# Layer 1's FFN down product as seven block products instead of eight

## The chip, the cores and the metric

The program runs on one core of one Trainium2 chip. The core has five engines that each work through their own list of instructions and meet only at semaphores: TensorE (PE, with its weight loads shown as PEld), VectorE (DVE), ScalarE (ACT), GpSimd (POOL) and SyncE (SP, which here only issues DMAs). The metric is the device time of one execution in microseconds (us); lower is better. A step of 512 columns through the 128x128 array is called a matmul below. Everything is computed in fp32 from three products of rounded parts: an operand is split into a high part (a cast to fp32r) and a low part (the rest), and hi·hi, hi·lo and lo·hi are summed in PSUM. One 128x128x512 block product is therefore three matmuls.

## What is computed

Two layers (DEPTH = 2) over 1024 latent tokens of width 1024, each an attention mixer and a feed-forward block with a convolution over tokens:

```python
def conv_ffn(h, w_up, conv_w, conv_b, w_down):
    u = h @ w_up                                  # 1024 x 1024 @ 1024 x 5632
    ...
    for j in range(CONV_W):                       # 3 taps along the tokens
        acc = acc + up[:, j:j + L] * conv_w[j]
    a, g = jnp.split(acc, 2, axis=-1)             # 2816 + 2816
    return (jax.nn.silu(g) * a) @ w_down          # 1024 x 2816 @ 2816 x 1024

# per layer, latent stream:
x = layer_norm(DN_ALPHA * x + m[2] * mixer(x), ...)
x = layer_norm(DN_ALPHA * x + m[5] * conv_ffn(modulate(x, m[3], m[4]), ...), ...)
```

The change is in the last part of the last layer: the product of the gated hidden values (1024 x 2816, that is 22 blocks of 128 hidden columns) with `w_down`.

## The kernel before

Layer 1's feed-forward block is one call of `ffn2` and ends the program. It has two phases.

**Up phase.** A loop of 22 passes (`p`), one per hidden block. Each pass makes the 128 `a` and the 128 `g` columns of its block by seven block products of 12 matmuls (`product`, L1689) into the PSUM tiles x, v, y, x, q, y, q: this product already goes by seven in place of eight. In the order of PE: W[0] into x, W[1] into v, W[4] into y, W[2] into x, W[5] into q, W[6] into y, W[3] into q. Beside it ACT casts the next pass's weights to their high parts (L1661), DVE takes the low parts (L1663) and the sums of weight blocks (L1665, L1668), ACT and DVE assemble the halves of `ua` and `ug` from the PSUM tiles (L1912, L1929 on ACT; L1921 and L1927 on DVE), and one pass later the convolution of the finished block runs: its centre tap on ACT (L1784), its side taps on DVE (L1792), SiLU on ACT (L1815), the gate product on DVE (L1818), and POOL issues the store of the 128x1024 block to `g` in DRAM (L1819). SP loads a pass's weights (L1642).

**Down phase.** 44 steps of 24 matmuls (`mm3`, L399 to L401): 22 hidden blocks for the left 512 output columns, then 22 for the right ones, each step over eight token tiles `t` with one PSUM bank each. `load` (L1763 for two blocks of `w_down`, L1767 for one block of `g`) brings a step's operands up to 8 steps ahead, and ACT and DVE split them (L110 and L111 for weights, L1773 and L1774 for `g`). The residual rows `z` come in (L1972) and are scaled (L1975, L1976). After the first 22 steps the banks are multiplied by the gate row (L1994) and added to `z` (L1962, with `bn_stats` in L1963). The last 8 steps are turned around: for each token tile in turn all 8, and then its evict (L2024, L1962, L1963) and its final norm, `finish_o`: L355 `bn_aggr`, two tiny POOL operations for the inverse deviation (L357, L358), two 128x1024 DVE operations (L2418, L2421) and the store to `out`, issued by SP (L2422).

The order of every engine's instructions is the order in which the code emits them, up to small moves by the framework's scheduler outside the parts marked `manual_schedule`; queues are served in order.

## Time and profile before

| quantity | value |
|---|---|
| median of 3 runs | 2938.8 us (2936.71 to 2944.41) |
| profiled execution | 2939.45 us |
| its span | 2937.7 us |
| mean granted TensorE clock | 0.98 |
| busy PE / DVE / ACT / POOL | 2788.0 / 2042.8 / 1365.4 / 635.5 us |
| up phase of layer 1 | ends at 2686 us from the span's start |
| down phase of layer 1 | 2686 to 2937.7 us |

In rows of the trace the first number is the start in us from the span's start, the second the duration; then engine, line, operation, output <- inputs, and in brackets the engine's idle time before it and what it waited for. Consecutive instructions overlap: the next one often starts before the printed end of the last. "x2" behind a row joins two instructions.

### The profile page before, as it was taken

The page shows a single profiled execution, that of the slowest core. Times are in us where ns is not written, and L with a number is a line of the kernel's source. Part 1 is how long each engine was busy: PE and PEld are TensorE (multiplying, and loading weights), DVE is VectorE, ACT ScalarE, POOL GpSimd, SP SyncE. Part 2 cuts the span into 40 slices and gives each one's busy share as a digit, 9 for nine tenths or more (in the row PEclk, how much of TensorE's full clock was granted, in tenths as well). Part 3 has the DMA queues.
Part 4 walks back from the last instruction along what each step waited for, and adds up shares of the span by engine and source line. Part 5 has one row for each costly group of instructions (what it writes and reads, how often), then busy time and mean ns, then how long its engine had stood idle before and what let it go on. Part 6 is the DMA issues. An engine that isn't in the chain of part 4 may idle for free.

```text
span 2937.7 us, 44921 instructions
## 1 busy us (share of the span) xinstructions
PE 2788.0 (95%) x16728; PEld 2276.0 (77%) x16728; DVE 2042.8 (70%) x3749; ACT 1365.4 (46%) x2594; POOL 635.5 (22%) x864
## 2 busy tenths in 40 slices
PE   7999899989999999999999978989998999999998
PEld 4877677778788978888888867766676788888886
DVE  4866366666578778888887566467767777777656
ACT  4321255567336655555553352267743555555330
POOL 2601233354450000000001023345543000000001
PEclk9999999999999999999999999989999999999999
DMA  8568611042667643333387427632144222225651
GB/s 263 156 193 273 215 39 34 9 157 74 171 186 224 202 153 107 119 112 113 101 302 240 144 92 228 190 95 65 52 151 158 77 75 86 86 79 189 241 161 61
DMA packets 347378, 416.47 MB, mean 142 GB/s; under 512 B 23432, under 2 KB 262312, under 8 KB 345624
## 3 DMA queue, kind: packets, MB, share of 16 engines
q1 hardware_dynamic: 326776, 351.31, 38.5%
q0 software_dynamic: 17488, 60.60, 6.0%
q8 instruction: 131, 2.15, 0.3%
q10 hardware_dynamic: 2896, 1.70, 0.2%
q14 instruction: 87, 0.71, 0.1%
HBM read 317.79 MB, written 95.75 MB: 141 GB/s over the span
## 4 chain that ended last, share of the span: by engine, by line
PE 71%; issue 9%; DVE 8%; DMA 6%; ACT 4%; POOL 1%; SPq 0%; ACTq 0%; POOLq 0%; DVEq 0%
PE q L1689 8%; PE x L1689 8%; PE y L1689 8%; PE d L399 5%; PE d L401 5%; PE d L400 5%; PE S L760 4%; PE v L1689 4%; PE pv L905 3%; PE T L891 3%; PE mm L399 2%; PE mm L401 2%; PE mm L400 2%; PE T L856 2%; PE pv L865 2%
## 5 line engine op out<-in xcount | busy, mean ns | idle before, releaser
L784 POOL TENSOR_SCALAR P<-P,rin 128x640 f32<-128x640 f32 (+3 forms) x288 | 249.5, 870 | 348.6 <-DVE rin L783 322.6
L1663 DVE TENSOR_TENSOR w<-raw,w 128x512 fp32r<-128x512 f32 x308 | 208.0, 688 | 143.1 <-ACT w L1661 143.0
L399 PE MATMUL d<-w,w 128*128 128x512 f32 x704 | 275.1, 391 | 0.0
L400 PE MATMUL d<-w,w 128*128 128x512 f32 x704 | 274.7, 390 | 0.0
L401 PE MATMUL d<-w,w 128*128 128x512 f32 x704 | 274.5, 390 | 0.0
L110 ACT CAST w<-raw 128x512 fp32r<-128x512 f32 x276 | 161.1, 620 | 185.2 <-PE d L401 128.1
L111 DVE TENSOR_TENSOR w<-raw,w 128x512 fp32r<-128x512 f32 x260 | 169.0, 691 | 97.3 <-ACT w L110 95.1
L760 PE MATMUL S<-k,q 64*128 64x256 f32 (+2 forms) x1824 | 192.9, 338 | 17.7 <-DVE nm L2248 9.2
L1819 POOL DMA_DIRECT2D g<-cv x44 | 23.5, 534 | 845.0 <-DVE cv L1818 845.0
L781 ACT ACTIVATE P<-P,nm 128x641 f32<-128x641 f32 (+4 forms) x208 | 161.3, 777 | 84.2 <-DVE nm L2248 46.9
L1661 ACT CAST w<-raw 128x512 fp32r<-128x512 f32 x308 | 182.0, 621 | 13.8 <-DVE raw L1668 7.9
L760 PEld LDWEIGHTS S<-k,q 64*128 64x128 f32 x1824 | 136.5, 189 | 53.4 <-issue 18.5
L771 ACT COPY PT<-T 128x512 f32<-128x512 f32 (+1 forms) x250 | 134.2, 567 | 77.6 <-PE T L891 75.4
L401 PEld LDWEIGHTS d<-w,w 128*128 128x128 f32 x704 | 132.6, 188 | 27.8
L400 PEld LDWEIGHTS d<-w,w 128*128 128x128 f32 x704 | 132.5, 188 | 27.5
L399 PEld LDWEIGHTS d<-w,w 128*128 128x128 f32 x704 | 132.5, 188 | 27.2
L905 PE MATMUL pv<-PT,v 128*64 128x128 f32 x2016 | 133.6, 280 | 16.7 <-ACT PT L771 13.8
L1774 DVE TENSOR_TENSOR w<-raw,w 128x512 fp32r<-128x512 f32 x176 | 112.3, 687 | 49.9 <-ACT w L1773 49.8
L891 PE MATMUL T<-ident,P 128*128 128x128 f32 x1008 | 136.1, 282 | 7.8 <-POOL P L784 3.4
L905 PEld LDWEIGHTS pv<-PT,v 128*64 128x64 f32 x2016 | 109.4, 138 | 42.5 <-ACT PT L771 22.3
L1929 ACT COPY ug<-q 128x512 f32<-128x512 f32 x44 | 25.9, 589 | 245.3 <-PE q L1689 245.3
L1773 ACT CAST w<-raw 128x512 fp32r<-128x512 f32 x176 | 98.8, 618 | 84.1 <-PE d L401 70.1
(364 smaller groups left out, 7566.2 us busy)
## 6 DMA issues: line engine op xcount, KB each, us to landing
raw<-in_up_dram SPq DMA_DIRECT2D x132, 512.0 KB
raw<-g SPq DMA_DIRECT2D x88, 512.0 KB
raw<-in_down_dram SPq DMA_DIRECT2D x66, 512.0 KB
g<-cv POOLq DMA_DIRECT2D x44, 512.0 KB, 3.0
araw<-in_ada_w_dram SPq DMA_DIRECT2D x32, 512.0 KB
raw<-in_w_in_dram SPq DMA_DIRECT2D x28, 512.0 KB
araw<-in_ada_w_dram SPq DMA_DIRECT2D x40, 256.0 KB
wt<-in_ada_w_dram SPq DMA_DIRECT2D x16, 512.0 KB
```

Of the source, the lines that this page charges most:

```text
L111: (lo_eng or nc.vector).tensor_sub(lo, s, f32(hi))
L399: nc.tensor.matmul(ps, lh, rh, start=first, stop=False)
L400: nc.tensor.matmul(ps, lh, rl, start=False, stop=False)
L401: nc.tensor.matmul(ps, ll, rh, start=False, stop=last)
L760: self.nc.tensor.matmul(outs[a], q[r, x, qs], k[r, y, ks], start=(i == 0), stop=(i == 2))
L781: nc.scalar.activation(P[:, :m], P[:, :m], AF.Exp, bias=negm, scale=-1.0, accum_out=den)
L784: nc.gpsimd.tensor_scalar(P[:, :n], P[:, :n], rin, 1.0, ALU.mult, ALU.mult)
L891: nc.tensor.transpose(ps[:, s * 128 : (s + 1) * 128], P[a][:, cols[i + x] : cols[i + x] + 128], self.ident,)
L905: nc.tensor.matmul(O[a * HD : (a + 1) * HD], v_of(a, vts[i + x]), pT[:, s * 128 : (s + 1) * 128], start=(i + x == 0), stop=(i + x == m - 1 ...
L1661: nc.scalar.copy(half(i, 0), src[i])
L1663: nc.vector.tensor_sub(half(i, 1), src[i], f32(half(i, 0)))
L1689: nc.tensor.matmul(ps, w[:, a, s], r[b][:, k], start=first and k + i == 0, stop=k == 3 and i == 2, skip_group_check=True,)
```

## The change

A new function, `ffn7`, takes the place of `ffn2` for layer 1 (layer 0 keeps `ffn2`). With the gated values in two token halves by two hidden halves, A11, A12, A21, A22 (hidden halves of 11 blocks), and `w_down` in two hidden halves by two column halves, W11, W12, W21, W22, it makes seven products in this order:

| steps | left factor (G) | right factor | PSUM banks | after it |
|---|---|---|---|---|
| 0 to 10 | S1 = A21 + A22 | V: T1 = W12 - W11 | Y | copy Y to `vs` (SBUF) |
| 11 to 21 | A11 | W11 | X | copy X to Y |
| 22 to 32 | A12 | W21 | X, summed on | X is the left columns of token tiles 0 to 3 |
| 33 to 43 | S2 = S1 - A11 | V: T2 = W22 - T1 | Y, summed on | copy Y to X |
| 44 to 54 | S4 = A12 - S2 | W22 | Y, summed on | Y + `vs` is the right columns of tiles 0 to 3 |
| 55 to 65 | S3 = A11 - A21 | V: T3 = W22 - W12 | X, summed on | X + `vs`: right columns of tiles 4 to 7; copy X to Y |
| 66 to 76 | A22 | V: W21 - T2 | Y, summed on | Y: left columns of tiles 4 to 7 |

A step is now 12 matmuls over four token tiles; there are 77 steps. X and Y are four PSUM banks each, and the copies are done by ACT.

The up phase visits the hidden blocks in pairs, one of each half (ORDER: 0, 11, 1, 12 and so on). The convolution results of a pair are the tiles `gk` and `go`. In place of one 512 KB store per block, a pair makes seven 256 KB stores to `G`, and DVE makes S1 in `store`, S3, S2 and S4 in `mix`, in place: each sum overwrites a half that an earlier store reads. The gate product stays one 128x1024 instruction. The weight sums are made by a generator, `mix_down`, that is advanced four times per pass: per pair of blocks five loads of 256 KB on SP, four DVE subtractions and four 256 KB stores to `V` on POOL, 77 advances in all, so that it is through in the 20th of the 22 passes.

In the down phase a `load` brings two steps: 512 KB of the right factor, 512 KB of G, two casts and two subtractions of 128x512 for the right factor, and from load 3 on one cast and one subtraction of 128x1024 for G. Loads lead by at most 6. The jobs of `evict` and `end` (the final norm and store of a token tile) for tiles 0 to 3 stand between steps 55 and 62; the evicts of tiles 4 to 7 (right columns) stand at steps 66 and 67; the last nine steps are turned around by token tile, four of them now.

Two small rows (`gq`, `gk` of the attention, no relation to the tile `gk`) move from one pool to another, so that their two DMAs on SP stand behind eight loads of `x` at the program's start.

```diff
+ORDER = [f + h for f in range(NF // 4) for h in (0, NF // 4)]
+            ("G", [7 * NF // 4, 128, 512]), ("V", [NF, 128, 512]),
...
+    def mix_down(self, tp, l):
+        nc, V = self.nc, self.d["V"]
+        w = self.io["down"][l].rearrange("(f p) n -> p f n", p=128)
+        HF = NF // 4
+        def load(tag, i, n):
+            r = self.t(tp, [128, 512], tag)
+            nc.sync.dma_start(r, w[:, f + i * HF, n * 512 : (n + 1) * 512])
+            return r
+        def sub(o, x, y, i):
+            nc.vector.tensor_sub(o, x, y)
+            nc.gpsimd.dma_start(V[i * HF + f], o)
+        for f in range(HF):
+            a, b = load("va", 1, 1), load("vb", 0, 1)
+            yield
+            sub(a, a, b, 2)
+            yield
+            a = load("va", 0, 0)
+            yield
+            sub(a, b, a, 0)
+            b = load("vb", 1, 1)
+            yield
+            sub(b, b, a, 1)
+            yield
+            a = load("va", 1, 0)
+            yield
+            sub(a, a, b, 3)
+            yield
...
+            def right(s, m):
+                q, f = divmod(s, HF)
+                if q in (0, 3, 5, 6):
+                    o = (0, 3, 5, 6).index(q) * HF + f
+                    return Vv[:, o : o + m]
+                o, n = {1: (0, 0), 2: (HF, 0), 4: (HF, 1)}[q]
+                return dn[:, o + f : o + f + m, n * 512 : (n + 1) * 512]
+            def raw():
+                rp.append(rp.pop(0))
+                return self.t(rp[0], [128, 2, 512], "raw")
+            def load(j):
+                s, m = 2 * j, min(2, 7 * HF - 2 * j)
+                if m <= 0:
+                    return
+                r, g = raw(), raw()
+                if m == 2 and (s + 1) % HF == 0:
+                    nc.sync.dma_start(r[:, :1], right(s, 1))
+                    nc.sync.dma_start(r[:, 1:], right(s + 1, 1))
+                else:
+                    nc.sync.dma_start(r[:, :m], right(s, m))
+                nc.sync.dma_start(g[:, :m], Gv[:, s : s + m])
+                for i, w in enumerate(self.split([r[:, i] for i in range(m)], 512)):
+                    wd[s + i] = w
+                if j < 3:
+                    for i, w in enumerate(self.split([g[:, i] for i in range(m)], 512)):
+                        ga[s + i] = w
+                    return
+                w = self.t(gp[0], [128, 2, 2, 512], "w", R)
+                nc.scalar.copy(w[:, 0, :m], g[:, :m])
+                nc.vector.tensor_sub(w[:, 1, :m], g[:, :m], f32(w[:, 0, :m]))
+                for i in range(m):
+                    ga[s + i] = w[:, :, i]
+            side = self.mix_down(up, l)
...
+                def a1(s):
+                    s.a = centre("go" if s.i % 2 else "gk", s.u[0], s.p)
+                def a2(s):
+                    sides(s.a, s.u[0], s.p)
+                def g1(s):
+                    s.g = centre("cv", s.u[1], s.p + NP)
+                def g2(s):
+                    sides(s.g, s.u[1], s.p + NP)
+                def silu(s):
+                    nc.scalar.activation(s.g, s.g, AF.Silu)
+                def store(s):
+                    f, x = s.i // 2, s.a
+                    nc.vector.tensor_mul(x, x, s.g)
+                    if s.i % 2 == 0:
+                        half["k"] = x
+                        put(1, f, x[:, :512])
+                        return
+                    put(2, f, x[:, :512])
+                    put(6, f, x[:, 512:])
+                    k = half["k"]
+                    nc.vector.tensor_add(k[:, 512:], k[:, 512:], x[:, 512:])
+                    put(0, f, k[:, 512:])
+                def mix(s):
+                    f, x, k = s.i // 2, s.a, half["k"]
+                    if s.i % 2 == 0:
+                        nc.vector.tensor_sub(k[:, :512], k[:, :512], k[:, 512:])
+                        put(5, f, k[:, :512])
+                        return
+                    nc.vector.tensor_sub(x[:, 512:], x[:, 512:], k[:, :512])
+                    put(3, f, x[:, 512:])
+                    nc.vector.tensor_sub(x[:, :512], x[:, :512], x[:, 512:])
+                    put(4, f, x[:, :512])
...
+                    call("h", 4)
+                    call("l", 3)
+                    c.store()
+                    nc.vector.tensor_tensor(v1, u1, cols(Q), ALU.add)
+                    next(side, None)
+                    self.product(W[6], b22, Y, False)
+                    call("l", 4)
+                    call("s", 5)
+                    call("s", 6)
+                    nc.vector.tensor_tensor(u1, u1, cols(Y), ALU.add)
+                    self.product(W[3], T[3], Q, False)
+                    nc.scalar.copy(v0, cols(Q))
+                    call("h", 5)
+                    call("h", 6)
+                    c.mix()
+                    next(side, None)
+                    c = conv(ua, ug, p)
+                    W, late_l = W2, call
+                for _ in side:
+                    pass
+                load(1)
+                for x in (c.a1, c.g1, c.a2, c.g2, c.silu, c.store, c.mix):
+                    x()
...
+            gp[0] = es.enter_context(self.pool("fgs", bufs=6))
...
+            X, Y = ([self.t(pd, [128, 512], f"d{x}{t}") for t in range(4)] for x in "xy")
+            banks = (Y, X, X, Y, Y, X, Y)
+            NS = 7 * HF
+            last = 9
+            def mm(i, t):
+                q, f = divmod(i, HF)
+                c = slice(t * 128, t * 128 + 128)
+                for k, (a, b) in enumerate(((0, 0), (0, 1), (1, 0))):
+                    nc.tensor.matmul(
+                        banks[q][t], ga[i][:, a, c], wd[i][:, b],
+                        start=q < 2 and f + k == 0, stop=f == HF - 1 and k == 2,
+                        skip_group_check=True,
+                    )
+            def evict(t, n, ps, v=None):
+                s = slice(n * 512, (n + 1) * 512)
+                tt = self.t(tt2, [128, 512], "tt")
+                if v is None:
+                    nc.vector.tensor_mul(tt, ps, gate[:, s])
+                else:
+                    nc.vector.tensor_add(tt, v, ps)
+                    nc.vector.tensor_mul(tt, tt, gate[:, s])
+                nc.vector.tensor_add(z[t][:, s], z[t][:, s], tt)
+                nc.vector.bn_stats(s6[t][:, n], z[t][:, s])
...
+            def end(t):
+                finish(t, z[t], s6[t])[0]()
...
+            def copies(dst, src):
+                for a, b in zip(dst, src):
+                    nc.scalar.copy(a, b)
+            job(HF - 1, copies, vs, Y)
+            job(2 * HF - 1, copies, Y, X)
+            job(4 * HF - 1, copies, X, Y)
+            job(6 * HF - 1, copies, Y, X)
+            for t in range(4):
+                job(3 * HF + 1 + 2 * t, evict, t, 0, X[t])
+                job(5 * HF + 2 * t, evict, t, 1, Y[t], vs[t])
+                job(5 * HF + 1 + 2 * t, end, t)
+                job(6 * HF + t // 2, evict, 4 + t, 1, X[t], vs[t])
+            ahead = 2
+            for i in range(NS - last):
+                if i % 2 == 0:
+                    n = i // 2 + min(5, 2 + i // 4)
+                    while ahead <= n:
+                        load(ahead)
+                        ahead += 1
+                for t in range(4):
+                    mm(i, t)
+                for f in jobs.pop(i, ()):
+                    f()
+            for t in range(4):
+                for i in range(NS - last, NS):
+                    mm(i, t)
+                evict(4 + t, 0, Y[t])
+                end(4 + t)
...
-        self.ffn2(1, h2l, [hl, pxc], {}, d["T1"], rows("x3"), a[1, 0, 5], view1, begin_o, finish_o,
-                  (io["ln_g"][1, 0], io["ln_b"][1, 0]), early=self.early, px=px, last=8, share=(9, (1, 4, 7)))
+        self.ffn7(1, h2l, [hl, pxc], {}, d["T1"], rows("x3"), a[1, 0, 5], view1, begin_o, finish_o,
+                  (io["ln_g"][1, 0], io["ln_b"][1, 0]), early=self.early, px=px)
```

On SP, at the end of the program, before (in these rows `raw` is a load's staging tile, `z` a token tile's 128x1024 rows, and the number behind a name tells tiles apart):

```order
L1763 DMA raw_28050<-in_down_dram 128x2x512
L1767 DMA raw_28058<-g_97 128x1024
L1767 DMA raw_28090<-g_97 128x1024
L157 DMA lg_28126<-in_ln_g_dram 128x1024
L157 DMA lb_28127<-in_ln_b_dram 128x1024
L2422 DMA out_dram<-z_4958_26675 128x1024
L2422 DMA out_dram<-z_4959_26676 128x1024
```

and after, in the same place (L2813 is the store of a token tile, L2120 and L2121 are the two DMAs of a load; the rows are load 33 to load 38):

```order
L2120 DMA raw_28148<-V_101 128x2x512
L2121 DMA raw_28149<-G_100 128x2x512
L2813 DMA out_dram<-z_5009_26958 128x1024
L2120 DMA raw_28198<-V_101 128x2x512
L2121 DMA raw_28199<-G_100 128x2x512
L2813 DMA out_dram<-z_5010_26959 128x1024
L2120 DMA raw_28248<-V_101 128x2x512
L2121 DMA raw_28249<-G_100 128x2x512
L2813 DMA out_dram<-z_5011_26960 128x1024
L2120 DMA raw_28298<-V_101 128x2x512
L2121 DMA raw_28299<-G_100 128x2x512
L2813 DMA out_dram<-z_5012_26961 128x1024
```

Before, no store of `out` stood ahead of a load; now four do, one ahead of each of the loads 34 to 37.

On DVE after, between two of these stores (L113 and L2130 take the low parts of load 34, L2362 to L2365 are the evict of a token tile, L357, L2809 and L2812 its final norm):

```order
L2812 SCALAR_TENSOR_TENSOR z_5009_26958<-z_5009_26958,rs_28175,lb_27618 128x1024
L2362 TENSOR_TENSOR tt_28193<-v_5026_26975,dy_5040_26995 128x512
L2363 TENSOR_TENSOR tt_28193<-tt_28193,gate_26978 128x512
L2364 TENSOR_TENSOR z_5010_26959<-z_5010_26959,tt_28193 128x512
L2365 BN_STATS s_5018_26967<-z_5010_26959 128x6
L113 TENSOR_TENSOR w_28202<-raw_28198,w_28202 128x512
L113 TENSOR_TENSOR w_28205<-raw_28198,w_28205 128x512
L2130 TENSOR_TENSOR w_28208<-raw_28199,w_28208 128x1024
L357 BN_AGGR mv_28223<-s_5018_26967 128x2
L2809 SCALAR_TENSOR_TENSOR z_5010_26959<-z_5010_26959,mv_28223,lg_27617 128x1024
L2812 SCALAR_TENSOR_TENSOR z_5010_26959<-z_5010_26959,rs_28225,lb_27618 128x1024
```

The low parts of load 34 stand ahead of the norm of token tile 1 in DVE's list; before, all splits stood ahead of every norm.

On ACT after, the end of the program (the last casts of loads 36 to 38, and the copies X to Y behind step 65):

```order
L112 CAST w_28302<-raw_28298 128x512
L112 CAST w_28305<-raw_28298 128x512
L2129 CAST w_28308<-raw_28299 128x1024
L112 CAST w_28347<-raw_28343 128x512
L112 CAST w_28350<-raw_28343 128x512
L2129 CAST w_28353<-raw_28344 128x1024
L2390 COPY dy_5039_26994<-dx_5035_26990 128x512
L2390 COPY dy_5040_26995<-dx_5036_26991 128x512
L2390 COPY dy_5041_26996<-dx_5037_26992 128x512
L2390 COPY dy_5042_26997<-dx_5038_26993 128x512
L112 CAST w_28388<-raw_28384 128x512
L2129 CAST w_28391<-raw_28385 128x512
```

Before, ACT's list ended in casts and had no copy that PE waits for in the down phase; now the copies that step 66 sums on stand behind the three casts of load 37.

On DVE in the up phase, before, from the gate product of one pass to the next pass's first split (L1818 the gate product, L1921 the half `v1`, which frees the PSUM tile q, L1927 the half `u1`):

```order
L1818 TENSOR_TENSOR cv_25009<-cv_25009,cv_25030 128x1024
L1921 TENSOR_TENSOR ug_24990<-ua_24989,q_4744_24987 128x512
L1663 TENSOR_TENSOR w_25083<-raw_24888,w_25083 128x512
L1668 TENSOR_TENSOR raw_24888<-raw_24888 128x512
L1668 TENSOR_TENSOR raw_24886<-raw_24886,raw_24888 128x512
L1927 TENSOR_TENSOR ua_24989<-ua_24989,y_4743_24986 128x512
L1663 TENSOR_TENSOR w_25118<-raw_24888,w_25118 128x512
```

and after, in a pass whose convolution ends a pair:

```order
L2181 TENSOR_TENSOR go_25153<-go_25153,cv_25174 128x1024
L2189 TENSOR_TENSOR gk_25004<-gk_25004,go_25153 128x512
L2305 TENSOR_TENSOR ug_25134<-ua_25133,q_4775_25131 128x512
L1665 TENSOR_TENSOR w_25231<-raw_25020,w_25231 128x512
L1670 TENSOR_TENSOR raw_25020<-raw_25020 128x512
L1670 TENSOR_TENSOR raw_25018<-raw_25018,raw_25020 128x512
L2311 TENSOR_TENSOR ua_25133<-ua_25133,y_4774_25130 128x512
L2198 TENSOR_TENSOR go_25153<-go_25153,gk_25004 128x512
L2200 TENSOR_TENSOR go_25153<-go_25153 128x512
L2050 TENSOR_TENSOR va_25240<-va_25240,vb_25242 128x512
L1665 TENSOR_TENSOR w_25273<-raw_25020,w_25273 128x512
```

S1 (L2189) now stands between the gate product and `v1` (L2305), S2 and S4 (L2198, L2200) and a weight sum (L2050) ahead of the next pass's split.

180 lines of the change are left out of this document (175 added, 5 removed).

## The prediction

> **What bounds the kernel now.** I read the page first, then the windows of the two phases of layer 1's feed-forward block, the chain of waits and the groups by line, and from there single stretches of the timeline. In this order, from these views:
>
> ```profile
> span 2937.7 us, 44921 instructions
> PE 2788.0 (95%) x16728; PEld 2276.0 (77%) x16728; DVE 2042.8 (70%) x3749; ACT 1365.4 (46%) x2594; POOL 635.5 (22%) x864
> ...
> 2252.00:2686.00 434.00, 422.82 (x1837) 347.26 (x1838) 321.33 (x409) 224.72 (x348) 13.66 (x24) 0.98 0.30 92
> 2686.00:2937.70 251.70, 239.45 (x1057) 197.94 (x1055) 159.28 (x223) 75.69 (x132) 15.12 (x17) 0.98 0.48 170
> ...
> 2506.57 2.72 PE q L1689 x12
> ...
> L400 PE MATMUL d<-w,w 128*128 128x512 f32 x352 | 136.9, 389 | 0.0
> ```
>
> PE is busy 95% of the span. The third and fourth rows are the up and the down phase (length; busy us and count of PE, PEld, DVE, ACT, POOL; clock; DMA share; GB/s). In the down phase PE's matmuls fill 239.45 of 251.7 us, and the group row shows 0.0 us of idle time ahead of them. The chain row gives the pitch: 12 matmuls in 2.72 us, 0.2267 us each. So a matmul taken away there is worth its pitch, as long as nothing else becomes late. What follows the last matmuls, in the timeline of the phase's end:
>
> ```profile
> 2887.41 0.69 DVE L2024 TENSOR_TENSOR tt<-d,gate 128x512 f32<-128x512 f32 x1 [8.93 <-PE d L401]
> 2888.13 0.69 DVE L1962 TENSOR_TENSOR z<-z,tt 128x512 f32<-128x512 f32 x1
> ...
> 2889.59 0.21 DVE L355 BATCH_NORM_AGGREGATE mv<-s 128x2 f32<-128x12 f32 x1
> 2889.83 1.28 DVE L2418 SCALAR_TENSOR_TENSOR z<-z,mv,lg 128x1024 f32<-128x1024 f32 x1
> 2891.85 1.28 DVE L2421 SCALAR_TENSOR_TENSOR z<-z,rs,lb 128x1024 f32<-128x1024 f32 x1 [0.73 <-POOL rs L358]
> 2893.05 0.68 DVE L2024 TENSOR_TENSOR tt<-d,gate 128x512 f32<-128x512 f32 x1
> ...
> 2926.78 0.68 DVE L2024 TENSOR_TENSOR tt<-d,gate 128x512 f32<-128x512 f32 x1
> ...
> 2931.20 1.28 DVE L2421 SCALAR_TENSOR_TENSOR z<-z,rs,lb 128x1024 f32<-128x1024 f32 x1 [0.71 <-POOL rs L358]
> ```
>
> Per token tile DVE needs 5.64 us (2887.41 to 2893.05); the norm alone, from `bn_aggr` to the end of L2421, is 3.54. The last evict and norm take 2926.78 to 2932.48, 5.70 us, and the span ends 5.2 us later with the last store. I count times from the down phase's start (2686.0); before, the last norm ends at +246.5.
>
> **The change, part by part.**
>
> *Matmuls.* 44 x 24 = 1056 become 77 x 12 = 924: 132 x 0.2267 = 29.9 us less, the whole of the possible gain.
>
> *The stores of tiles 0 to 3 among the loads.* How much of it is lost is decided by these rows, the waits of SP's queue (us in total, times, longest) and single rows of the timeline:
>
> ```profile
> SPq L2422 <- DVE z L2421: 69.5, 8, 33.0
> ...
> SPq L1642 <- DVE w L1663: 450.8, 39, 18.7
> ...
> 2724.91 0.32 SPq L1767 DMA_DIRECT2D raw<-g  x1
> 2726.16 0.32 SPq L1972 DMA_DIRECT2D z<-x  x1
> ...
> 2731.49 0.38 SPq L1763 DMA_DIRECT2D raw<-in_down_dram  x1
> ...
> 2734.75 1.15 ACT L110 CAST w<-raw 128x512 fp32r<-128x512 f32 x2 [1.52 <-DMA raw<-in_down_dram]
> ...
> 2507.09 1.07 ACT L1815 ACTIVATE cv<-cv 128x1024 f32<-128x1024 f32 x1
> ...
> 2517.49 0.57 ACT L1887 COPY y<-x 128x512 f32<-128x512 f32 x1 [1.09 <-PE x L1689]
> ...
> 2509.30 1.22 DVE L1818 TENSOR_TENSOR cv<-cv,cv 128x1024 f32<-128x1024 f32 x1
> 2510.44 0.68 DVE L1921 TENSOR_TENSOR ug<-ua,q 128x512 f32<-128x512 f32 x1
> ```
>
> SP waits at an instruction until its releaser is done, up to 33.0 us for the norm ahead of a store. Before, all stores stood behind all loads, and this cost nothing. Now a store of tile t waits on DVE for norm t, load 34 + t stands behind it on SP, load 34 + t's splits stand on DVE ahead of norm t + 1. That is a ring: each turn must run through in series.
>
> One turn, from the end of norm t: the load is issued at once behind the store; from issue to first cast 3.26 us (2731.49 to 2734.75); the store's own 512 KB go ahead, one more slot of 1.25 (2724.91 to 2726.16); G comes one slot later, 1.25; its 128x1024 cast 1.07 (the SiLU row is the nearest of that size), its low part 1.22 (the gate product's row), the norm 3.54. Sum 11.6 us, in which PE does two steps, 5.44. The evict (2.9 of DVE) fits into the wait for data.
>
> First turn: load 33's casts reuse tiles that steps 54 and 55 read, so they start when step 55 ends, at 56 x 2.72 = +152.3. One 128x512 cast 0.57, then 1.07, 1.22 and 3.54: norm 0 ends at +158.7. Norm 3 ends three turns later, at +193.5.
>
> PE meanwhile runs on loaded data to step 66, at 66 x 2.72 = +179.5. There it needs the copies X to Y, which stand on ACT behind load 37's casts, and load 37 is behind the fourth store: its G is cast at 193.5 + 3.26 + 1.25 + 1.25 + 1.07 = +200.3, the first copy takes 0.57 more (the later ones have the 0.68 that PE spends per tile). PE waits there from +179.5 to +200.9, 21.4 us. A restart is slow at first, as the timeline shows behind an earlier wait:
>
> ```profile
> 2300.68 0.69 PE L1689 MATMUL q<-T3h,w 128*128 128x512 f32 x1 [2.97 <-DVE ug L1921]
> ...
> 2304.89 0.39 PE L1689 MATMUL q<-T3h,w 128*128 128x512 f32 x1
> 2305.12 0.40 PE L1689 MATMUL x<-h3lah,w 128*128 128x512 f32 x1
> ```
>
> After this idle of 2.97 us, 12 matmuls took 4.44 us (2300.68 to 2305.12) in place of 2.72: 1.7 us. I take that once; the bounds are 0 and twice that. Steps 66 to 76 are 11 x 2.72 = 29.9, then the last evict and norm 5.7: the last norm ends at 200.9 + 1.7 + 29.9 + 5.7 = +238.2. DVE is through with the evicts of tiles 4 to 7 by then (about 202 + 4 x 2.9 = +214). Against +246.5 the down phase gains 8.3 us out of 29.9.
>
> A rule of the Trainium skill would make the ring shorter. "DMA: Bandwidth & Descriptors", section "Two DMAs through the same engine are not ordered", has it that in one queue transfers start in order but are pipelined, with reading and writing on separate queues. Then the load's reads need not wait for the store's slot, and three turns lose 3 x 1.25 us. No row here shows a store followed by a load on SP.
>
> *The first copies* (behind steps 10, 21, 43) have no late load ahead of them; each takes 0.57 against PE's 0.68 per tile: nothing; bounds 0 and 4 x 0.57 each.
>
> *The sums in the up phase.* 44 sums of halves (S1 to S4 of 11 pairs) and 44 weight sums, all 128x512, at DVE's pitch of about 0.6 us. Per pass 44 / 19.25 = 2.3 weight sums and 1 or 3 sums of halves: 2.0 or 3.2 us. These must fit DVE's gaps, in the timeline of one pass (and W[3] in the chain):
>
> ```profile
> 2500.74 2.60 DVE L1792 SCALAR_TENSOR_TENSOR cv<-ua,cc,cv 128x1023 f32<-128x1023 f32 x2 [0.46 <-ACT cv L1784]
> ...
> 2508.69 0.69 DVE L1663 TENSOR_TENSOR w<-raw,w 128x512 fp32r<-128x512 f32 x1 [1.03 <-ACT w L1661]
> ...
> 2515.91 1.29 DVE L1663 TENSOR_TENSOR w<-raw,w 128x512 fp32r<-128x512 f32 x2 [2.38 <-ACT w L1661]
> ...
> 2518.63 0.69 DVE L1663 TENSOR_TENSOR w<-raw,w 128x512 fp32r<-128x512 f32 x1 [0.82 <-ACT w L1661]
> ...
> 2512.01 2.72 PE q L1689 x12
> ```
>
> The gaps of a pass of 19.04 us are 0.46 + 1.03 + 2.38 + 0.82 = 4.7 us, all spent on ACT, so late work is caught up there. The tight place is `v1`, which frees q for W[3]: it ends at 2511.12, PE starts W[3] at 2512.01, 0.89 us later. S1 ahead of it takes 0.6 of that; the weight sum ahead of it falls into the 1.03. So I take 0 per pass; the bounds are 0 and 2.6 - 0.9 = 1.7 us per pass (all the added work late at `v1`). Only in pass 0, where DVE has no such gap, does a weight sum delay W[3]: +0.6 us.
>
> *The new transfers* are 256 KB each: per pair 7 stores and 9 transfers for the weight sums in place of 2 stores. In that phase the DMA share is 0.30 (first fence), so there is room; SP's weight loads for a pass are issued a pass ahead. Zero; bounds 0 and 0.2 per pass.
>
> *Between the phases* S2 and S4 of the last pair wait until earlier stores have landed (the page's DMA issues, with the us to landing, and the timeline):
>
> ```profile
> g<-cv POOLq DMA_DIRECT2D x44, 512.0 KB, 3.0
> ...
> 2697.32 1.23 DVE L1818 TENSOR_TENSOR cv<-cv,cv 128x1024 f32<-128x1024 f32 x1 [1.19 <-ACT cv L1815]
> ...
> 2698.84 0.53 POOL L1819 DMA_DIRECT2D g<-cv  x1 [16.55 <-DVE cv L1818]
> ```
>
> The second store of the pair would be issued about 2699.4 and land 3.0 later, +16.4. In DVE's new list the splits of loads 2 and 3 stand ahead of S2, so steps 4 to 7 have their data: zero. Behind S2 and S4 (1.2) and with their own four (2.4), load 2 would be ready at +20, 9 us after step 4's turn at +10.9: bounds 0 and 9.
>
> *The two small rows* leave SP's queue ahead of `x` (two slots of 1.25), but DVE then waits for them: 0; bounds -2.5 and +1.
>
> **Sum**: -8.3 + 0.6 = -7.7 us. The profiled execution took 2939.45, 0.65 over the median, so I set the sum against the median: 2938.8 - 7.7 = 2931.1. What a measurement can tell from no change is 0.3%, 8.8 us: below 2930.0 counts as faster, above 2947.6 as slower.
>
> **The rivals.**
> - *Reads pass the store*: a load's first data come as if no store stood ahead, turns of 10.35 us, norm 3 at +189.8, so 2927.4. Against it: the rows of transfers issued one after the other, 1.25 us apart; for it: none of those rows mixes the two directions. The Trainium skill's rule above would give this case.
> - *Stores do not hold the loads.* Then load 37 is early, the copies come at step 66 on time, and DVE bounds: per tile splits 2.4, norm 3.5, evict 2.9, so norm 3 at 158.7 + 3 x 8.8 = +185.1; splits of loads 37 and 38 (3.7) and four evicts to +200.4; then four times 5.64 to +223.0, 23.5 less: 2915.9. Against it speaks the 33.0 us wait of SP at a store.
> - *The store holds the rings longer*: with 3.0 us (the put's landing) for 1.25 a turn is 13.35, 2936.4; with the 5.2 us behind the last norm 15.6, about 2943. It loses to before from a turn of 14.2 on.
> - *DVE falls behind in the up phase* (the slower side): `v1` late in each pass because the sums don't fall into the gaps. It becomes slower than before from 7.7 / 22 = 0.35 us per pass, by over 0.3% from 0.75; at 0.8 the time is 2948.7. For it: the margin at `v1` is 0.3 us in every second pass; against: 4.7 us of gaps ahead of it.
>
> **How the numbers follow.** The forecast 0.45, reads pass 0.10, stores don't hold 0.12, longer store 0.14, DVE behind 0.19. The predicted time is the forecast's, 2931; its own range, a turn shorter or longer by 1 us and a clock term of 0 to 3.4, is 2926 to 2936. The range over the cases leaves out stores that don't hold (0.12) and the upper part of DVE behind (0.07): 2921 to 2950. Faster: 0.17 of the forecast, 0.09, 0.12: 0.38. Slower: 0.15 of DVE behind, 0.02 of the longer store: 0.17. Same: 0.45.
>
> **What would show it.** In the trace after: one PE wait of about 21 us ahead of step 66, ended by ACT's copies; SP waits for norms 0 to 3, about 11.6 us apart; DVE's low part of load 34 + t some 8 us behind norm t; a low clock for some us after the wait; passes of 19.04 us as before; no PE wait at steps 0 to 65. A pass over 19.4 us, a wait at step 4, or copies on time at step 66 would make the forecast wrong.

## The result, and the profile after

The changed kernel is slower: 2953.24 us median (2949.12 to 2955.11, 4 runs) against 2937.76 for the kernel before (4 runs beside it); the ratio is 1.0049, 95% interval 1.0026 to 1.0072. The prediction had it 0.26% faster, and its range ended at 2950.

The page of the changed kernel, and the windows of the same two phases (length; busy us and count of PE, PEld, DVE, ACT, POOL; clock; DMA share; GB/s):

```profile
span 2949.7 us, 45178 instructions
...
PE 2771.6 (94%) x16596; PEld 2256.5 (77%) x16596; DVE 2118.9 (72%) x3832; ACT 1382.9 (47%) x2597; POOL 688.6 (23%) x963
...
2252.00:2686.00 434.00, 419.85 (x1803) 341.96 (x1804) 371.46 (x493) 223.84 (x347) 65.19 (x119) 0.98 0.53 166
2686.00:2949.70 263.70, 222.73 (x958) 182.63 (x957) 183.98 (x226) 94.60 (x137) 18.36 (x23) 0.92 0.56 194
```

132 matmuls are gone, PE is 16 us less busy, and the span is 12.0 us longer. Where PE waits now stands in the timeline of PE; these are its three largest waits behind 2290 us:

```profile
2306.24 0.79 PE L1691 MATMUL q<-T3h,w 128*128 128x512 f32 x1 [3.58 <-DVE ug L2305]
...
2757.58 17.59 PE L2350 MATMUL dx<-w,w 128*128 128x512 f32 x65 [3.73 <-ACT dy L2390]
...
2905.27 20.11 PE L2350 MATMUL dy<-w,w 128*128 128x512 f32 x78 [25.16 <-ACT dy L2390]
```

The first stood there before (2.97 us). The other two are new, and both end with ACT's bank copies (L2390): ahead of step 22 and ahead of step 66. Ahead of the third the ring can be read, in the timeline of SP, ACT and DVE:

```profile
2870.32 1.28 DVE L2812 SCALAR_TENSOR_TENSOR z<-z,rs,lb 128x1024 f32<-128x1024 f32 x1 [0.72 <-POOL rs L360]
...
2871.63 0.35 SPq L2813 DMA_DIRECT2D out_dram<-z  x1
2872.08 0.39 SPq L2120 DMA_DIRECT2D raw<-V  x1
2872.55 0.79 SPq L2121 DMA_DIRECT2D raw<-G  x1
...
2877.19 1.15 ACT L112 CAST w<-raw 128x512 fp32r<-128x512 f32 x2 [10.29 <-DMA raw<-V]
2878.48 1.05 ACT L2129 CAST w<-raw 128x1024 fp32r<-128x1024 f32 x1
...
2882.95 1.28 DVE L2812 SCALAR_TENSOR_TENSOR z<-z,rs,lb 128x1024 f32<-128x1024 f32 x1 [0.72 <-POOL rs L360]
...
2895.20 1.28 DVE L2812 SCALAR_TENSOR_TENSOR z<-z,rs,lb 128x1024 f32<-128x1024 f32 x1 [0.72 <-POOL rs L360]
...
2904.64 2.03 ACT L2390 COPY dy<-dx 128x512 f32<-128x512 f32 x4
```

Norm, store, load, casts, norm: one turn takes 12.6 us here (2870.32 to 2882.95), 12.4 on average from norm 0 (2857.95) to norm 3 (2895.20).

The span's 12.0 us divide as follows. "Start" of the phase is the end of the chain's last `PE q` row: 2686.09 before (2683.37 + 2.72) and 2693.70 after (2690.97 + 2.73).

| stretch | before | after | difference | forecast |
|---|---|---|---|---|
| up to the transposes ahead of the up phase | 2236.79 | 2239.09 | +2.3 | 0 |
| from there to W[0] behind the third row above | 68.5 | 71.5 | +3.0 | +0.6 |
| up phase from there to its end | 380.81 | 383.14 | +2.3 | 0 |
| down phase to the end of the last norm | 246.39 | 249.66 | +3.3 | -8.3 |
| from there to the span's end | 5.2 | 6.3 | +1.1 | 0 |

(W[0] starts at 2305.28 before and 2310.56 after, in the chain; the last norm ends at 2932.48 and 2943.36.)

Part of the second row is the clock. Behind a wait of 1.84 us before and 1.83 us after, the 5 us from PE's restart read as follows in the windows, first before, then after (the clock is the third number from the end):

```profile
2257.50:2262.50 5.00, 3.50 (x14) 2.55 (x14) 4.97 (x7) 2.62 (x5) 1.67 (x1) 1.00 0.44 166
...
2259.80:2264.80 5.00, 4.90 (x12) 3.87 (x13) 4.97 (x8) 1.10 (x3) 1.66 (x1) 0.51 0.46 168
```

Within the down phase, counted from its start, the forecast and the trace compare so:

| point | forecast | measured |
|---|---|---|
| end of norm 0 | +158.7 | +165.5 |
| end of norm 3 | +193.5 | +202.8 |
| PE goes on at step 66 | +200.9 | +211.6 |
| end of the last norm | +238.2 | +249.7 |

### The profile page after: what moved, and what is told of

It reads as the page before. It is cut to its first block, busy times and chain, and to the rows that moved or that the text cites. A ratio compares the mean times of both kernels' runs of the same rounds, so it can differ in the third digit from the quotient of the medians.

```text
span 2949.7 us, 45178 instructions
## 1 busy us (share of the span) xinstructions
PE 2771.6 (94%) x16596; PEld 2256.5 (77%) x16596; DVE 2118.9 (72%) x3832; ACT 1382.9 (47%) x2597; POOL 688.6 (23%) x963
## 4 chain that ended last, share of the span: by engine, by line
PE 68%; issue 9%; DMA 9%; DVE 8%; ACT 5%; POOL 1%; SPq 1%; ACTq 0%; DVEq 0%; POOLq 0%
PE x L1691 8%; PE q L1691 8%; PE y L1691 8%; PE S L762 5%; PE v L1691 4%; PE pv L907 3%; PE T L893 3%; PE dy L2350 3%; PE d L403 2%; PE d L402 2%; PE d L401 2%; PE mm L401 2%; PE mm L402 2%; PE mm L403 2%; PE pv L867 2%
## 5 line engine op out<-in xcount | busy, mean ns | idle before, releaser
L112 ACT CAST w<-raw 128x512 fp32r<-128x512 f32 x315 | 183.0, 620 | 208.4 <-PE d L403 61.0
L1665 DVE TENSOR_TENSOR w<-raw,w 128x512 fp32r<-128x512 f32 x308 | 207.3, 687 | 84.1 <-ACT w L1663 84.0
L113 DVE TENSOR_TENSOR w<-raw,w 128x512 fp32r<-128x512 f32 x299 | 194.2, 689 | 92.7 <-ACT w L112 90.6
L1663 ACT CAST w<-raw 128x512 fp32r<-128x512 f32 x308 | 182.0, 621 | 13.9 <-DVE raw L1670 7.8
L2350 PE MATMUL dy<-w,w 128*128 128x512 f32 x528 | 122.7, 394 | 25.2 <-ACT dy L2390 25.2
L401 PE MATMUL d<-w,w 128*128 128x512 f32 x352 | 138.6, 394 | 0.0
L403 PE MATMUL d<-w,w 128*128 128x512 f32 x352 | 138.0, 392 | 0.0
L402 PE MATMUL d<-w,w 128*128 128x512 f32 x352 | 138.0, 392 | 0.0
L2350 PEld LDWEIGHTS dy<-w,w 128*128 128x128 f32 x528 | 100.5, 191 | 47.1 <-ACT dy L2390 25.6
L771 DVE COPY PT<-T 128x512 f32<-128x512 f32 (+1 forms) x166 | 110.4, 666 | 31.3 <-PE T L893 21.1
L893 PEld LDWEIGHTS T<-ident,P 128*128 128x128 f32 x1008 | 110.2, 142 | 27.9 <-issue 14.1
L785 DVE RECIPROCAL rin<-den 128x1 f32<-128x1 f32 x288 | 46.0, 161 | 118.8 <-ACT P L783 116.2
L1691 PE MATMUL q<-T3h,w 128*128 128x512 f32 x352 | 118.2, 397 | 5.0 <-DVE ug L2305 4.2
L1691 PE MATMUL q<-T2h,w 128*128 128x512 f32 x352 | 115.9, 390 | 3.9 <-ACT q L1906 2.3
```

The lines of the kernel that those rows point to most:

```text
L112: nc.scalar.copy(hi, s)
L113: (lo_eng or nc.vector).tensor_sub(lo, s, f32(hi))
L401: nc.tensor.matmul(ps, lh, rh, start=first, stop=False)
L402: nc.tensor.matmul(ps, lh, rl, start=False, stop=False)
L403: nc.tensor.matmul(ps, ll, rh, start=False, stop=last)
L893: nc.tensor.transpose(ps[:, s * 128 : (s + 1) * 128], P[a][:, cols[i + x] : cols[i + x] + 128], self.ident,)
```

## The experiments

The theory at this point: the ring costs what PE waits at step 66; a second loss of the same kind, a full DMA queue ahead of step 22, comes on top; S1 ahead of `v1` and the two moved rows cost a few us each. The rivals: the copies are late for their place on ACT alone; the store's data, not SP's wait, holds the loads.

### Stores behind the loads (a_stores)

```diff
-                nc.sync.dma_start(io["out"][t * 128 : (t + 1) * 128, :], z)
+                held.append((t, z))
+                if t >= 4:
+                    while held:
+                        u, y = held.pop(0)
+                        nc.sync.dma_start(io["out"][u * 128 : (u + 1) * 128, :], y)
```

> Edit: the stores of token tiles 0 to 3 are issued behind the last load, everything else as in the changed kernel. If the ring store, load, splits, norm is the cause, norms 0 to 3 follow each other by DVE's own work (about 8.8 us apart in place of 12.4), PE's wait of 25.2 us ahead of step 66 is gone or under 3 us, and DVE bounds the end: norm 0 at +165.7 as measured, norm 3 at about +192, four evicts and the splits to about +207, then four times 5.64: last norm at about +230 in place of +249.8, so some 20 us less, about 2933. If the copies behind load 37's casts are late for another reason (their place on ACT, DMA rate), the wait at step 66 stays above 15 us and the time above 2945.

Measured: 2933.6 us (10 runs) against 2942.04 for the kernel before on that chip (13 runs), ratio 0.9977 (0.9965 to 0.9989). By the two ratios to before (1.0049 and 0.9977) the edit is worth 0.72%, 21 us. The norms in DVE's timeline:

```profile
2853.36 1.28 DVE L2812 SCALAR_TENSOR_TENSOR z<-z,rs,lb 128x1024 f32<-128x1024 f32 x1 [0.73 <-POOL rs L360]
...
2861.91 1.28 DVE L2812 SCALAR_TENSOR_TENSOR z<-z,rs,lb 128x1024 f32<-128x1024 f32 x1 [0.72 <-POOL rs L360]
...
2879.01 1.28 DVE L2812 SCALAR_TENSOR_TENSOR z<-z,rs,lb 128x1024 f32<-128x1024 f32 x1 [0.72 <-POOL rs L360]
...
2916.11 1.28 DVE L2812 SCALAR_TENSOR_TENSOR z<-z,rs,lb 128x1024 f32<-128x1024 f32 x1 [0.72 <-POOL rs L360]
```

They are 8.55 us apart, and of PE's waits in the down phase only that ahead of step 22 is left (3.2 us). The last norm ends at +226.9 (2917.39 from 2690.54). So the ring is the cause of the wait at step 66, and moving four DMA issues turns the change from 0.5% slower to 0.2% faster.

### The same stores issued by POOL (l_pool)

```diff
-                nc.sync.dma_start(io["out"][t * 128 : (t + 1) * 128, :], z)
+                (nc.gpsimd if t < 4 else nc.sync).dma_start(io["out"][t * 128 : (t + 1) * 128, :], z)
```

> Edit: the stores of tiles 0 to 3 stay where they are in the program, but POOL issues them in place of SP; nothing else. If it is SP's wait at a store that holds the loads, norms 0 to 3 are 8.5 to 9 us apart, as with the stores behind the loads, PE has no wait ahead of step 66, and the last norm ends +226 to +229 from the phase's start (+226.9 with the stores behind the loads, +249.8 in the changed kernel). If it is the store's data on the DMA engines that hold the loads' data, norms are over 10 us apart and the last norm is later than +232.

Measured: 2927.47 us (one run; before 2935.44 there). The waits of PE in the down phase (total, times, longest):

```profile
PE dx L2350 <- ACT dy L2390: 3.2, 1, 3.2
```

Norms 8.56 us apart (2854.94, 2863.50), last norm at +226.9 again. The stores move the same data at the same place in the work; the issuing list differs, and with it the DMA queue. That it is SP's list which held the loads shows in the issue of load 37, first in the changed kernel, then with the stores on POOL:

```profile
2896.95 0.39 SPq L2120 DMA_DIRECT2D raw<-V  x1
```

```profile
2860.23 0.36 SPq L2120 DMA_DIRECT2D raw<-V  x1
```

From the phase's start that is +203.3, right behind the store of tile 3, against +168.1. The ring is made by SP's wait; what the store's data adds to a turn is not separated by this run.

### Two of the four stores among the loads (m_two)

```diff
-                if t >= 4:
+                if t < 2 or t >= 4:
```

(on top of the first edit)

> Edit: only the stores of tiles 0 and 1 stay among the loads, those of 2 and 3 go behind the last load. If each store left in place makes one slow turn, norms 1 and 2 come 12.5 us behind the one before, norm 3 some 8.6; DVE then ends at about +199 + 3.7 + 11.6 + 22.5 = +237 (half of the way between +249.8 and +226.9), with a short PE wait ahead of step 66 (some 8 us). If one store is enough, the last norm stays above +245; if only the last one counts, it is below +230.

Measured: 2935.1 us (one run; before 2935.44 there). Norms 1 and 2 came 12.65 and 12.50 us behind the one before, norm 3 only 8.55; the wait ahead of step 66 was 5.7 us, the last norm at +235.3. Each store left among the loads makes one slow turn of its own.

### The copies ahead of load 37's casts (b_copy)

```diff
                     n = i // 2 + min(5, 2 + i // 4)
+                    if i < 6 * HF:
+                        n = min(n, 36)
                     while ahead <= n:
```

> Edit: loads 37 and 38 are emitted behind step 65, so that ACT's copies stand ahead of load 37's casts; the stores stay where they are. If the ring is the cause, norms 0 to 3 stay about 12.4 us apart, the copies come when evict 3 has read its bank (about 3 us behind norm 2, some 16 us earlier), but PE then waits for load 37 at step 74, some 7 us, and DVE with its late evicts bounds the end: within 5 us of the changed kernel, 2948 to 2954. If the place of the copies alone is the cause, both waits are under 3 us and the time is below 2940.

Measured: 2947.62 us (one run; before 2942.04 there). The waits of PE in the down phase:

```profile
PE dy L2350 <- ACT dy L2390: 12.6, 1, 12.6
PE dx L2350 <- ACT dy L2390: 3.2, 1, 3.2
PE dy L2350 <- DVE w L2130: 0.4, 1, 0.4
```

Half of the wait is gone, and the last norm came only 3.9 us earlier from the phase's start (+245.8). The norms stayed 12.4 to 12.7 us apart, and behind them DVE had the four late evicts and four norms of 5.62 each to do. The expected second wait, 7 us at step 74, was 0.4. So the place of the copies is not the cause by itself: freeing PE without freeing DVE's chain buys little.

### Residual rows loaded later (c_zlate)

```diff
-                job(6 + t, lambda t: nc.sync.dma_start(z[t], xsrc(t)), t)
-                job((18 + 2 * t) if t < 4 else (42 + 2 * (t - 4)), scale, t)
+                job(22 + 2 * t, lambda t: nc.sync.dma_start(z[t], xsrc(t)), t)
+                job((28 + 2 * t) if t < 4 else (42 + 2 * (t - 4)), scale, t)
```

> Edit: the eight loads of residual rows start at step 22 in place of step 6 (tiles 0 to 3 are scaled at steps 28 to 34). If PE's wait of 3.7 us at step 33's bank copies (X to Y behind step 21) comes from a DMA queue that is full in steps 6 to 22, the wait is gone, the matmuls behind it run at full clock, and norm 0 ends some 5 to 7 us earlier from the phase's start (+159 to +161 in place of +165.7); the ring behind it stays, so the whole is 5 to 7 us less. If the wait comes from the wait of SP for a store of G between the phases, it stays at 2 us or more.

(The wait stands ahead of step 22, the first of X's second product; the copies read X behind step 21.) Measured: 2949.82 us (one run; before 2942.04 there). PE's waits in the down phase, the only row:

```profile
PE dy L2350 <- ACT dy L2390: 25.3, 1, 25.3
```

The wait ahead of step 22 is gone, norm 0 ended at +159.0 and the last norm at +243.7, 6 us earlier, with the ring as before. In the changed kernel the windows of 10 us around that wait read:

```profile
2723.00:2733.00 10.00, 10.00 (x46) 8.29 (x45) 4.95 (x6) 4.97 (x8) 0.00 (x0) 1.00 1.04 393
...
2743.00:2753.00 10.00, 10.00 (x45) 8.26 (x44) 6.69 (x9) 6.07 (x9) 0.00 (x0) 1.00 1.04 387
2753.00:2763.00 10.00, 6.27 (x17) 4.64 (x16) 9.93 (x12) 7.30 (x12) 0.00 (x0) 0.66 0.84 305
```

In the first two the DMA engines are fully busy (share 1.04) at about 390 GB/s: the lead of the loads grows from 2 to 6 there, the eight residual rows add 4 MB, and SP had lost 7.0 us to a wait for a store of G just before, as its waits show:

```profile
SPq L2121 <- DMA G<-gk: 7.0, 1, 7.0
```

ACT's copies behind step 21 stand behind casts of loads that are late. The chain of waits of the changed kernel runs through a residual row (`z`) there:

```profile
2725.72 11.40 DMA z<-x
2737.18 10.61 DMA raw<-G
...
2751.42 5.17 DMA raw<-in_down_dram
2757.58 32.78 PE dx L2350 x132
```

SP's wait for the store of G is still there in c_zlate (7.5 us), where PE doesn't wait, so it is the residual rows and not that store. Full engines alone don't make PE wait either: c_zlate reads 1.04 in the window 2743 to 2753, and the kernel before 1.03 from 2710 to 2740, both without a wait of PE. What counts is which transfers stand ahead of the loads that the copies sit behind. The clock of the last of the three windows (0.66) shows the second part of the price.

### S1 behind v1 (e_s1)

```diff
-                    k = half["k"]
-                    nc.vector.tensor_add(k[:, 512:], k[:, 512:], x[:, 512:])
-                    put(0, f, k[:, 512:])
...
                     nc.vector.tensor_tensor(v1, u1, cols(Q), ALU.add)
+                    c.s1()
```

(`s1` holds the three lines for the second block of a pair.)

> Edit: the sum S1 of a pair and its store stand behind the half v1 on DVE in place of ahead of it. If S1's place is what lengthens every second pass of the up phase (W[3] took 2.90 to 3.02 us in place of 2.72 there), all W[3] rows behind the first three passes are 2.72 long and the stretch from the first W[0] behind the wait near 2306 us to the down phase is 2 to 4 us shorter than in the changed kernel (383.1 us there, 380.8 before). If the sums as a whole or the new transfers are the cause, the stretch stays above 382.5.

Measured: 2946.36 us (one run; before 2940.38 there). In the changed kernel the chain shows every second W[3] long:

```profile
2666.32 2.72 PE q L1691 x12
2669.03 2.72 PE y L1691 x12
2671.75 2.90 PE q L1691 x12
```

Ten such rows of 2.90 to 3.02 us stood behind the restart (2.3 us over 2.72 in all); with the edit two of 3.04 are left. The stretch, though, is 382.2 us, 0.9 less where 2 to 4 were expected: the restart's slow clock reached into it in that run (its first W[0] took 2.91), and the two remaining waits take a part. In g_all and k_fold below, which have this edit too, the same stretch took 382.7 and 381.7. The place of S1 is shown as the cause of the long rows; what the edit is worth, between 0.5 and 2.3 us, these runs don't settle.

### The two small rows (d_rows, h_before_rows)

In the first the rows of the changed kernel go back ahead of `x`; in the second the kernel before gets the move and nothing else. The edit of the second:

```diff
-        gq, gk = (self.t(self.cst, [128, HD], "g" + n) for n in "qk")
...
-            self.bcast(gq, io["qg"][0])
-            self.bcast(gk, io["kg"][0])
             load_x(0, 0)
...
         tab = e1.enter_context(self.pool("tab"))
+        gq, gk = (self.t(tab, [128, HD], "g" + n) for n in "qk")
+        self.bcast(gq, io["qg"][0])
+        self.bcast(gk, io["kg"][0])
```

> Edit: the two small rows of the attention are loaded ahead of the x loads again, as in the kernel before (in a small pool of their own). If the moved rows cost the 2.3 us by which the changed kernel is late before layer 1's feed-forward block, POOL's tables stand near 31 us again in place of 38 to 45, DVE's casts of 128x512 beside them take 0.43 us in place of 1.47, the first matmuls of the projection start near 41.4 in place of 46.3, and every later stage is 2.3 us earlier (1.5 to 3). If not, the lateness at 2239 us stays.

> Edit: the kernel before, with the two small rows of the attention moved behind the x loads, as the change has them, and nothing else. If the move alone makes the start late, POOL's tables stand near 38 to 45 us, DVE's casts beside them take about 1.47 us in place of 0.43, the first matmuls of the projection start at 43 and 46 us in place of 40.6 and 41.4, and layer 1's feed-forward block begins 0 to 5 us later than before. If the rest of the change made it late, the rows are as before.

Measured: 2947.52 and 2943.78 us (one run each). Timeline of DVE, POOL and PE at the start, first the kernel before, then the same with the rows moved:

```profile
38.91 0.43 DVE L542 CAST hh<-sg 128x512 fp32r<-128x512 f32 x1 [0.35 <-ACT sg L533]
...
30.91 1.26 POOL L553 TENSOR_TENSOR tbq<-rp,gq 128x512 f32<-128x512 f32 x1 [29.62 <-DMA gk<-in_kg_dram]
32.14 1.41 POOL L561 TENSOR_TENSOR tbq<-rp,gq 128x256 f32<-128x256 f32 x2
...
41.36 0.38 PE L400 MATMUL mm<-w,hh 128*128 128x256 f32 x1 [0.34 <-DVE w L111]
```

```profile
38.75 1.40 DVE L542 CAST hh<-sg 128x512 fp32r<-128x512 f32 x1 [0.29 <-ACT sg L533]
...
38.60 1.26 POOL L553 TENSOR_TENSOR tbq<-rp,gq 128x512 f32<-128x512 f32 x1 [37.30 <-DVE gq L549]
39.83 2.03 POOL L561 TENSOR_TENSOR tbq<-rp,gq 128x256 f32<-128x256 f32 x2
...
46.75 0.58 PE L400 MATMUL mm<-w,hh 128*128 128x256 f32 x1 [2.25 <-DVE w L111]
```

In all eight profiles of kernels with the move the second matmul of the projection stands at 46.3 to 47.2 us, in the four without it at 41.2 to 41.6: 5 us, and the kernel before with only the rows moved shows that the move alone makes them. Both engines are slower where POOL's tables and DVE's casts coincide. How much of it lasts can't be told: in d_rows the transposes stood 2.2 us earlier than in the changed kernel, as expected, but over all profiles those transposes stand at 2235.4 to 2241.5 with the move and at 2234.0 to 2244.7 without (g_all and k_fold are in the latter), so the 2.3 us in the table above lie within what the attention stages vary by from run to run.

### All four edits, and less work for DVE at the end (g_all, k_fold)

`g_all` joins a_stores, c_zlate, d_rows and e_s1. `k_fold` adds:

```diff
+            def gated():
+                for t in range(4):
+                    nc.vector.tensor_mul(vs[t], vs[t], gate[:, 512:])
+            def fold(t):
+                nc.vector.tensor_add(z[t][:, 512:], z[t][:, 512:], vs[t % 4])
...
+            job(20, gated)
+            for t in range(NLAT):
+                job((29 + 2 * t) if t < 4 else (43 + 2 * (t - 4)), fold, t)
...
-                job(5 * HF + 2 * t, evict, t, 1, Y[t], vs[t])
+                job(5 * HF + 2 * t, evict, t, 1, Y[t])
...
-                job(6 * HF + t // 2, evict, 4 + t, 1, X[t], vs[t])
+                job(6 * HF + t // 2, evict, 4 + t, 1, X[t])
```

and starts the weight sums in pass 1 in place of pass 0.

> Edit: the four single edits together: stores of tiles 0 to 3 behind the loads, residual rows loaded from step 22 on, the two small rows ahead of x, S1 behind v1. If the four costs add, the changed kernel's 2953 loses 20 (stores, by a ratio of 0.993 as the first edit alone showed), 0 to 4 (residual rows; DVE bounds the end, so less than PE gains), 2.3 and 2 to 4: 2923 to 2928. If they were one and the same cost seen in different places, the time stays at that of the first edit alone, 2933.

> Edit: all of the former, and DVE's work at the end cut: the part of the right columns that both halves share (vs) is multiplied by the gate and added to the residual rows in steps 20 to 50, where DVE has time, so that eight late evicts take three operations in place of four; the weight sums begin one pass later. If DVE bounds the end once the ring is gone, the last norm comes 5 to 6 us earlier than in the former, and PE's own sum holds: the phase takes 209.4 + 5.7 = 215 to 219 us up to the last norm in place of 246.5 before, and the whole is 2914 to 2922. If something else bounds it, the time is that of the former.

Measured against the same nine runs of the kernel before (2940.38):

| kernel | us | ratio to before | last norm from the phase's start |
|---|---|---|---|
| before | 2940.38 | 1 | +246.4 |
| changed | 2953.24 | 1.0049 (1.0026 to 1.0072) | +249.7 |
| a_stores | 2933.6 | 0.9977 (0.9965 to 0.9989) | +226.9 |
| g_all | 2919.71 | 0.9928 (0.9914 to 0.9943) | +221.7 |
| k_fold | 2914.15 | 0.9908 (0.9892 to 0.9923) | +216.7 |

g_all came out 3 us under its expected band, k_fold at the edge of its own; the runs of the two overlap (2916.81 to 2924.23 and 2909.17 to 2921.92), so what k_fold adds is read from the down phase. (The changed kernel and a_stores were measured beside other runs of the kernel before, 2937.76 and 2942.04; the ratios compare.) The down phase of k_fold, from its start near 2697, as a window and in the chain of waits:

```profile
2697.00:2917.00 220.00, 209.72 (x924) 173.03 (x922) 180.91 (x225) 93.84 (x135) 17.31 (x21) 0.99 0.65 230
...
2696.95 30.25 PE dy L2360 x132
2727.20 59.84 PE dx L2360 x264
2787.04 57.13 PE dy L2360 x252
...
2912.37 1.28 DVE z L2832
```

PE's 924 matmuls take 209.7 us without a wait, and the chain is PE's up to 2844, then DVE's. The last four norms stand 5.62 us apart, DVE's own pitch, so DVE still ends last. The new operations cost nothing where they were put, and the 5.0 us by which k_fold's last norm is earlier than g_all's are the eight operations taken out of the end (seven of them stand behind norm 0, which comes at the same point: 7 x 0.72 = 5.0). The last norm is now 29.7 us earlier from the phase's start than before (246.4 to 216.7), as much as the 29.9 us of matmuls; the medians differ by 26.2, 0.9%.

## Why the prediction was wrong, point by point

- **The ring** was right in mechanism and under-sized. A turn was set at 11.6 us and took 12.4: SP spends 0.45 us on the store before it issues the load (2871.63 to 2872.08), which the sum left out, and the first cast came 5.1 us behind that issue where the sum had 3.26 + 1.25. Behind norm 3 load 37 needed 8.8 us to PE's restart in place of 7.4. In all PE waited 25.2 us for a forecast of 21.4. The rivals on this point fell: the turn of 10.35 us that reads passing the store would give did not come, stores do hold the loads, and by a_stores, l_pool and m_two it is SP's wait at the store that does it. The longer store was the nearest of the rivals in direction.
- **"The first copies ... have no late load ahead of them: nothing"** is the step that failed. The same order, copies behind casts on ACT, was worked out for step 66 and taken for granted behind step 21. What the sum left out are the eight residual rows that stand ahead of the loads in steps 6 to 22, on DMA engines that are already full. PE waited 3.7 us there and restarted at a low clock; norm 0 ended 6.8 us late against the sum, and the whole ring began that much later. With the eight rows moved (c_zlate), norm 0 came at +159.0, the forecast's +158.7, and the last norm 6 us earlier. This step is the largest, but not the whole: by this account 12.0 less 6.8 would still be 5.2 us slower than before.
- **The sums in the up phase** were set at 0 per pass with the margin at `v1` worked out as 0.3 us. The margin was not quite there: every second W[3] was 0.2 us late, and these rows add up to the 2.3 us of the stretch. The rival "DVE behind" was this mechanism at a third of its break-even.
- **The early up phase**: the weight sum's 0.6 us in pass 0 came as predicted (W[3] waited 0.61 there). Of the other 2.4 us, 0.6 are a second such delay, in the third PE wait (3.58 against 2.97; 2.97 again in k_fold, whose sums begin a pass later). About 1.6 are the slower clock shown above: from the transposes to PE's restart behind the product that ran at it (2264.68 before, 2268.54 after) it took 29.5 us in place of 27.9. Nine profiles with weight sums in pass 0 took 64.7 to 68.2 us between the transposes and the end of the third PE wait, against 63.9 in the first profile of the kernel before, 65.7 in that with only the rows moved, and 66.0 with the sums begun in pass 1. Just behind that restart the clock was 1.00 in a_stores (64.7) and 0.52 in k_fold (66.0), so it doesn't follow the change; why it is low in some profiles and full in others stays open.
- **The two small rows**: set at 0, between -2.5 and +1. The start lost 5 us at the projection by a mechanism that wasn't looked for, POOL's tables moving beside DVE's casts; whether it reaches the end stays open.
- **The clock** after PE's long wait: 1.7 us set, and about 2.5 found (32.4 us from the restart to the end of 132 matmuls in place of 29.9). The windows show 0.52 for the first 5 us and full speed from 2910 on.

In sum, the forecast of -8.3 us for the down phase missed by 11.6: 6.8 in front of norm 0, 2.5 in the turns, 1.4 behind norm 3, 0.8 of clock, and 0.1 because the forecast counted from 2686.0. The rest of the 19.7 us between the forecast and the spans is 2.3 and 1.8 us of stretches that vary between runs, 0.6 of the sums in the early up phase, 2.3 of S1, and 1.1 behind the last norm. That last stretch is 6.3 to 6.7 us long in every profile with the new down phase and 5.2 in both of the old one; its cause stays open.

**A store and a load on one queue.** The Trainium skill, "DMA: Bandwidth & Descriptors", section "Two DMAs through the same engine are not ordered", says that transfers of one queue start in order but are pipelined, with reading and writing on separate queues. In the turn shown above, the load behind a store of 512 KB had its first cast 5.1 us after its issue; the prediction's row without a store ahead had 3.26. That speaks for the store's data costing the load time, but the two rows are from different kernels and stages, the second with full DMA engines, and no run isolates it. With the stores on POOL's queue it did not show, since the loads were issued early enough.

## What to carry to other kernels

A store that waits for the last engine of a chain must not stand ahead of loads in an in-order issuing list, when the chain's engine has those loads' work ahead of its next piece: this closes a ring, and each store costs one full turn. When a loop is rewritten, go through every instruction that an engine waits at and list what stands behind it on that engine, for all places of the same form, not for the worst one alone. Count DMA demand stage by stage, and what stands ahead of the loads that matter: the phase's mean share of 0.56 hid 30 us at 1.04.

## What the runs showed of the hardware that had not been expected

DVE's cast of 128x512 to fp32r took 0.43 us alone and mostly 1.35 to 1.49 us beside POOL's table products (0.87 once, in m_two), POOL's 128x256 products took 1.41 us for two alone and 2.04 beside DVE, and two 128x512 subtractions of the same stretch went from 1.29 to 2.23. Two engines that share no instruction and no data slowed each other by up to a factor of 3.4, in all eight profiles of kernels with the move; in the four without it only the first cast, beside the end of POOL's tables, was slower (0.55 to 0.76). Moving two DMAs of 32 KB behind eight others was enough to bring them together.
